# Within a pair, the product of a22 between the second and the third sum's instead of ahead of both

## The chip, the cores and the metric

The kernel runs on one core of one Trainium2 chip. The metric is device time in microseconds (us), taken over whole executions. The kernel before takes 1060.31 us (median of 3 runs, 1059.55 to 1061.11).

## The reference

One decoder layer on 512 tokens and 16 learned meta tokens, width 2048, all in fp32. What is computed, cut to what matters here:

```python
u = rms_norm(h, norm_w)                       # h: 528 x 2048
proj = u @ w_in                               # w_in: 2048 x 8192, eight parts of 1024 columns
sb_q, sb_k, sb_v, sb_g, df_q, df_k, df_v, df_g = split(proj)
# 8 heads of stick-breaking attention (sb): a = exp(log_beta + tail sum of log_keep), masked; out = a @ v
# 8 heads of differential attention (df): q, k normed and rotated, w = softmax1 - lam * softmax2; out = w @ v
mixed = concat(sb_o * silu(sb_g), rms_norm(df_o) * silu(df_g))
y = mixed @ w_out                             # w_out: 2048 x 2048
h = h + y
```

The two projections are the bulk of the matrix work.

## The kernel before

**Pairs.** The 64 column blocks (128 columns each) of the input projection are taken two at a time as 32 pairs, numbered 0 to 31, the 16 blocks of the output projection as 8 pairs, 32 to 39. A pair is a product of a 2 x 2 block matrix of weights (two column blocks times the two halves of the depth; its four quarters are a11, a21, a12, a22) with a 2 x 2 block matrix of activations (two halves of the depth, two halves of the tokens). It is done with seven block products instead of eight, on sums of quarters: the activations' sums are made once (`combine`), the weights' for each pair. Pairs 2 to 31 (the in-pairs) and 33 to 39 (the out-pairs) go this way; pairs 0, 1 and 32 are multiplied directly.

**The seven products.** `STEPS` (L56) gives for each its PSUM bank and its activations: s1 into bank d, a11 into bank a, a12 into b, a22 into c, s2 and s3 *added onto* bank a, s4 into e. In the trace the banks of pair 34 are pj34a to pj34e. Each product is 8 blocks of depth (7 in the out-pairs), each three matmuls of 256 or 264 columns (high by high, high by low, low by high parts: L279, L280, L281). After a11, ScalarE copies bank a (ev_a, L470); after s2, VectorE reads bank a and writes u4 = a + m5 (ev_u, L523); after s3, ScalarE copies it again (ev_g). The first matmul of s3 writes bank a, so it has to wait for ev_u. The pair's results are formed with banks b, c, a and e by `final` (L478); in the out-pairs `final` first adds 6 matmuls each (`plain`, tiles w..pl) for the part of the depth left over.

**Order of products.** `uses(s)` (L227) lists them: s1, a11, then s4 of the pair before, a12, a22, s2, s3. `proj_pair` walks it. After each block of depth it ticks the attention work of the head before, which is interleaved with the products. The framework then plans all instructions with a simulated timeline: among those that it holds to be ready it takes the earliest in program order, with a boost for what stands under `hp`, and so fixes each engine's order and which buffer a tile takes. Engines then run their queues in that order.

**Weights.** `w_loads` loads the quarters of the next pair from SyncE's queue into tiles of 512 KB (wr.., six buffers). For the in-pairs the sums are made by accumulating DMAs from GpSimd's queue (`w_add`, L174), in place: s1 = a21+a22, then s2 = that + a11, then s4 = that + a12, in the tile of a21; s3 = a11+a21 in that of a11. The DMA of a sum is issued after the split of what stood in its tile before (`NEXT`): s2's after s1's split, s4's after s2's. For the out-pairs GpSimd adds (`OUT_SUMS`, L220): s1 in a21's tile, s2 in a11's, s3 = s2 - a22 in a21's, s4 in a12's. `w_prep` splits a weight tile into a high and a low part, two units each: ScalarE writes the high part (L124, w.._h), VectorE the low one (L125, w.._l), into a ring of four units. `preps` runs ahead of the products and prepares in the order of the same `uses(s)`, so the ring holds two products' weights. In the trace w34a_h stands for any of a11, a12, a22 and w34s_h for any sum.

Of the kernel before, what the change touches and what calls it, by code (L numbers as in the profile page):

```python
# [82 lines left out]
def build(nc, tc, ctx, hT, win, wout, wpl, xT, prm, cst, out):  # L83
# [142 lines left out]

    def uses(s):  # L227

        o = [(s, which) for which in ("s1", "a11", "a12", "a22", "s2", "s3")]
        if s - 1 > 1 and s - 1 not in (last_in, last_in + 1):  # L230
            o.insert(2, (s - 1, "s4"))
        if s in (last_in, len(plan) - 1):
            o.append((s, "s4"))
        return o

    def preps():


        for s in range(1, len(plan)):
            if s == last_in + 1:  # L240
                continue
            while (s, "a22") not in raw or (s, "a12") not in raw:
                yield
            if s == 1:
                for quads, _ in ROWS:
                    for u in range(2):
                        for which in quads:
                            w_half(s, which, u)
                            yield
                continue  # L250
            for t, which in uses(s):
                w_prep(t, which)
                yield
                if which == "a12" and s > last_in:
                    w_prep(s, "pl")
                    yield
# [195 lines left out]
    def proj_pair(s, dst, base=None, done=None):  # L452
# [50 lines left out]
        for t, which in uses(s):  # L503
            if which == "s4":
                if t == s:
                    yield from last()
                else:
                    yield from carried.pop(t)
                continue
            yield from multiplied(which)  # L510
            x = STEPS[which][0]
            if which == "a11":
                m1 = copied(x, "a")
                onto_base(0, 0, m1)
            elif which == "s1":
                m5 = copied(x, "d")
                onto_base(1, 1, m5)
            elif which == "a12":
                yield from final(x, 0, 0, m1)
            elif which == "s2":  # L520
                u4 = ev("u")
                with hp(offset=600):
                    V.tensor_tensor(u4, bank(x), m5, op=ALU.add)  # L523
                onto_base(0, 1, u4, ALU.subtract)
            elif which == "s3":
                u3 = copied(x, "g")
                onto_base(1, 0, u3, ALU.subtract)
                yield from final("c", 1, 0, u3, ALU.subtract)
                yield from final(x, 1, 1, m5)
# [436 lines left out]
    s = last_in + 1  # L966
# [142 lines left out]
```

## Time and profile before

| what | us |
|---|---|
| median of 3 runs | 1060.31 |
| the profiled execution's own time | 1060.54 |
| its span (first to last instruction) | 1058.8 |
| TensorE busy (PE) | 1017.8 |
| VectorE busy (DVE) | 832.1 |
| ScalarE busy (ACT) | 631.1 |
| GpSimd busy (POOL) | 432.2 |

The busy time of an engine is the union of its instructions. Of TensorE, ends of matmuls are modelled: a matmul of 256 columns shows some 0.28 us while the next starts 0.12 us later, so a short gap between starts does not show as idle time. The in-pairs run from some 60 to 845 us, pair 32 and the last attention from there to some 900, the out-pairs from there to the end.

### The profile page before, as it was taken

How to read it: one execution, taken by the hardware profiler on the slowest of the kernel's cores; microseconds unless marked ns; L12 is line 12 of the kernel's file. 1: busy time of each engine (PE TensorE's matmuls, PEld its weight loads, DVE VectorE, ACT ScalarE, POOL GpSimd, SP SyncE). 2: the span in 40 equal slices, each digit the busy share in tenths (PEclk: the TensorE clock that was granted, in tenths of full speed). 3: DMA queues.
4: the chain of work that ended last, by engine and by line, in shares of the span. 5: the costliest groups of instructions: out<-in, count | busy, mean ns of one | idle time of the engine just before them, and what ended most of it. 6: DMA issues, size and time to landing. Idle time of an engine off the chain costs nothing. (4 is left out here: it accounts for less than half of the span.)

```text
span 1058.8 us, 21804 instructions
## 1 busy us (share of the span) xinstructions
PE 1017.8 (96%) x8263; PEld 997.4 (94%) x8263; DVE 832.1 (79%) x1577; ACT 631.1 (60%) x1226; POOL 432.2 (41%) x374
## 2 busy tenths in 40 slices
PE   8899999999999999999999999999999987999998
PEld 7899999999999999999999999999999986899998
DVE  5978877878787878787868796878687999578766
ACT  9836665666565566566745674666566665344443
POOL 3544224323422352244224422432243265477574
PEclk9999999999999999999999999999999988999999
DMA  9346685777677767767776767676768535345431
GB/s 338 84 112 141 165 191 141 180 168 190 148 182 173 176 161 170 180 153 169 169 172 167 172 159 180 154 183 158 192 140 210 135 105 164 113 131 161 156 121 36
DMA packets 55113, 169.28 MB, mean 160 GB/s; under 512 B 6368, under 2 KB 7904, under 8 KB 55008
## 3 DMA queue, kind: packets, MB, share of 16 engines
q0 software_dynamic: 17280, 62.92, 33.9%
q1 hardware_dynamic: 37584, 104.96, 28.7%
q8 instruction: 65, 1.06, 0.4%
q14 instruction: 40, 0.33, 0.1%
q10 hardware_dynamic: 144, 0.01, 0.0%
HBM read 160.00 MB, written 7.86 MB: 159 GB/s over the span
## 5 line engine op out<-in xcount | busy, mean ns | idle before, releaser
L838 ACT ACTIVATE df_p<-df_s,df_mx,df_q_r 128x144 f32<-128x144 f32 (+3 forms) x64 | 40.2, 628 | 13.5 <-DVE df_mx L836 11.9
L749 POOL TENSOR_TENSOR df_o_r<-df_o_m,mhalf 128x8 f32<-128x8 f32 x8 | 13.7, 1714 | 57.3 <-DVE df_o_m L745 57.3
L710 DVE TENSOR_TENSOR_SCAN sb_r<-sb_k,ones 128x144 f32<-128x144 f32 (+3 forms) x32 | 29.3, 916 | 7.6 <-ACT sb_k L707 6.5
L835 DVE TENSOR_REDUCE df_mx<-df_s 128x1 f32<-128x144 f32 (+3 forms) x64 | 32.0, 500 | 3.3 <-PE df_s L833 3.3
L830 PE MATMUL df_s<-df_dk,df_qs 128*128 128x264 f32 (+3 forms) x80 | 24.4, 313 | 7.7 <-ACT df_p L838 7.7
L124 ACT ACTIVATE sb_ah<-sb_at 128x512 fp32r<-128x512 f32 (+4 forms) x40 | 18.0, 449 | 20.2 <-PE sb_at L631 18.5
L124 ACT ACTIVATE df_ah<-df_at 128x512 fp32r<-128x512 f32 (+4 forms) x40 | 17.7, 444 | 18.2 <-PE df_at L631 17.9
L707 ACT ACTIVATE sb_k<-sb_s,nrqs 128x144 f32<-128x144 f32 (+3 forms) x32 | 17.3, 541 | 17.6 <-PE sb_s L704 14.2
L830 PEld LDWEIGHTS df_s<-df_dk,df_qs 128*128 128x128 f32 x80 | 15.0, 188 | 10.4 <-ACT df_p L838 10.4
L631 PE MATMUL sb_at<-ident,a_all 128*128 128x128 f32 x112 | 20.8, 278 | 4.1 <-DVE a_all L712 4.1
L833 PE MATMUL df_s<-df_dk,df_qs 128*128 128x264 f32 (+3 forms) x80 | 23.7, 297 | 0.0
L125 DVE TENSOR_TENSOR sb_al<-sb_at,sb_ah 128x512 fp32r<-128x512 f32 (+4 forms) x40 | 20.0, 500 | 3.8 <-ACT sb_ah L124 3.4
L749 POOL TENSOR_TENSOR df_k_r<-df_k_m,mhalf 128x10 f32<-128x10 f32 x8 | 19.2, 2404 | 8.6 <-DVE df_k_m L748 8.5
L125 DVE TENSOR_TENSOR df_al<-df_at,df_ah 128x512 fp32r<-128x512 f32 (+4 forms) x40 | 19.8, 497 | 0.3
L733 POOL TENSOR_TENSOR df_q_sh<-df_q_sh,sin_t 128x512 f32<-128x512 f32 x8 | 12.4, 1552 | 18.3 <-DVE df_q_sh L732 18.3
L631 PE MATMUL df_at<-ident,a_all 128*128 128x128 f32 x112 | 19.8, 272 | 0.0
L712 DVE TENSOR_TENSOR a_all<-sb_b,sb_r 128x143 f32<-128x143 f32 (+3 forms) x32 | 18.0, 563 | 1.9
L279 PE MATMUL pj<-uth,w32a_h 128*128 128x256 f32 x56 | 16.1, 305 | 3.4 <-DVE o31b L487 3.4
L838 ACT ACT_TABLE_LOAD x7 | 9.0, 1283 | 17.5 <-DVE df_mx L836 17.5
L708 ACT ACTIVATE sb_b<-sb_s,rqs 128x144 f32<-128x144 f32 (+3 forms) x32 | 17.3, 539 | 2.8 <-DVE a_all L712 2.8
L631 PEld LDWEIGHTS sb_at<-ident,a_all 128*128 128x128 f32 x112 | 13.1, 137 | 5.8 <-DVE a_all L712 4.5
L832 PE MATMUL df_s<-zid,mdf 128*128 128x256 f32 x64 | 18.0, 281 | 0.0
(2599 smaller groups left out, 5354.3 us busy)
## 6 DMA issues: line engine op xcount, KB each, us to landing
xr<-in_xT SPq DMA_DIRECT2D x16, 256.0 KB, 3.4
out_dram<-xr SPq DMA_DIRECT2D x13, 256.0 KB, 2.0
wr0a<-in_win SPq DMA_DIRECT2D x8, 256.0 KB, 5.2
wr1a<-in_win SPq DMA_DIRECT2D x4, 512.0 KB, 7.3
wr2a<-in_win SPq DMA_DIRECT2D x4, 512.0 KB, 4.0
wr2a<-in_win POOLq DMA_DIRECT2D x4, 512.0 KB, 5.6
wr3a<-in_win SPq DMA_DIRECT2D x4, 512.0 KB, 3.5
wr3a<-in_win POOLq DMA_DIRECT2D x4, 512.0 KB, 7.1
```

The costliest lines, as they stand in the source:

```text
L124: S.activation(hi, src, AF.Copy)
L125: E.tensor_tensor(lo, src, hi.bitcast(F32), op=ALU.subtract)
L631: PE.transpose(pt[:kk, i * P:(i + 1) * P], a_t[i][:, b * P:b * P + kk], ident)
L707: S.activation(sview(keep, i), view, AF.Sigmoid, scale=nrqs[:, i:i + 1])
L710: V.tensor_tensor_scan(run[:, ::-1], keep[:, ::-1], ones_t.to_broadcast([P, n]), 1.0, op0=ALU.mult, op1=ALU.mult)
L712: V.tensor_tensor(a_t[i][:, :n - 1], beta[:, :n - 1], run[:, 1:], op=ALU.mult)
L749: G.tensor_tensor(r, m, mhalf[:, :2 * nb].rearrange("p (a c) -> p a c", c=2), op=ALU.pow)
L830: PE.matmul(o, qst[c][:, qs], dk[:, c, cs], start=True, stop=False)
L832: PE.matmul(diag[0], mdf, diag[1], start=False, stop=False)
L833: PE.matmul(o, qst[c][:, qs], dk[:, 2 + c, cs], start=False, stop=True)
L835: V.tensor_reduce(mxn, view, axis=AX.XY if i == 3 else AX.X, op=ALU.max, negate=True)
L838: S.activation(sview(pt, i), view, AF.Exp, bias=mxn, scale=rqn[:, i, c:c + 1], accum_out=sums[:, c:c + 1])
```

## The change

One line of `uses`: a22 moves behind s2.

```diff
     def uses(s):

-        o = [(s, which) for which in ("s1", "a11", "a12", "a22", "s2", "s3")]
+        o = [(s, which) for which in ("s1", "a11", "a12", "s2", "a22", "s3")]
         if s - 1 > 1 and s - 1 not in (last_in, last_in + 1):
             o.insert(2, (s - 1, "s4"))
```

As `preps` and `proj_pair` both walk this list, the order of the products and the order in which their weights are prepared change together: s2's weights are split one product earlier, a22's one later, the sum s4 (which waits for s2's split) can be issued earlier, and the tile of a22 is let go later. It holds for the 30 in-pairs and the 7 out-pairs. No instruction is added or taken away.

## Rows read from the trace of the kernel before

**Rows 1.** The page's busy times by engine: us, share of the span, instructions.
```profile
PE 1017.8 (96%) x8263; PEld 997.4 (94%) x8263; DVE 832.1 (79%) x1577; ACT 631.1 (60%) x1226; POOL 432.2 (41%) x374
```
**Rows 2.** Busy time by stretch: us, PE, PEld, DVE, ACT, POOL, granted clock, DMA share, GB/s.
```profile
410.00:510.00 100.00, 98.69 (x820) 97.14 (x820) 78.27 (x160) 61.78 (x120) 35.16 (x30) 1.00 0.72 171
...
942.00:963.00 21.00, 20.46 (x171) 20.29 (x171) 16.37 (x20) 9.56 (x18) 15.52 (x14) 1.00 0.50 161
```
**Rows 3.** Waits of TensorE: who waited for whom, us in total, times, longest.
```profile
PE df_s L830 <- ACT df_p L838: 7.7, 13, 0.9
...
PE pj31e L279 <- ACT w31s_h L124: 1.7, 1, 1.7
...
PE pj36a L279 <- DVE ev_u L523: 1.2, 1, 1.2
...
PE pj35a L279 <- DVE ev_u L523: 1.1, 1, 1.1
...
PE pj33a L279 <- ACT w34s_h L124: 0.6, 1, 0.6
```
**Rows 4.** Timeline of TensorE where s3 follows s2 (out-pairs 34, 35, 36).
```profile
941.49 0.28 PE L281 MATMUL pj34a<-uth,w34s_l 128*128 128x256 f32 x1
942.38 0.36 PE L279 MATMUL pj34a<-uth,w34s_h 128*128 128x256 f32 x1 [0.61 <-DVE ev_u L523]
...
963.90 0.36 PE L279 MATMUL pj35a<-uth,w35s_h 128*128 128x256 f32 x1 [1.06 <-DVE ev_u L523]
...
985.56 0.36 PE L279 MATMUL pj36a<-uth,w36s_h 128*128 128x256 f32 x1 [1.19 <-DVE ev_u L523]
```
**Rows 5.** Timeline of TensorE where s3 follows s2 in in-pair 18.
```profile
508.12 0.28 PE L281 MATMUL pj18a<-uth,w18s_l 128*128 128x264 f32 x1
508.24 0.28 PE L279 MATMUL pj19d<-uth,w19s_h 128*128 128x256 f32 x1
...
509.55 0.45 PE L830 MATMUL df_s<-df_dk,df_qs 128*128 128x400 f32 x1 [0.92 <-ACT df_p L838]
...
511.31 0.28 PE L279 MATMUL pj18a<-uth,w18s_h 128*128 128x264 f32 x1
```
**Rows 6.** Timeline of VectorE: splits of pair 34's a22, s2 and pair 35's s1.
```profile
934.55 2.72 DVE L125 TENSOR_TENSOR w34a_l<-wr34a,w34a_h 128x512 fp32r<-128x512 f32 x2
...
938.13 0.54 DVE L125 TENSOR_TENSOR w34s_l<-wr34a,w34s_h 128x384 fp32r<-128x384 f32 x1
...
943.44 0.83 DVE L125 TENSOR_TENSOR w35s_l<-wr35a,w35s_h 128x512 fp32r<-128x512 f32 x1 [1.21 <-ACT w35s_h L124]
```
**Rows 7.** SyncE's queue: the load of pair 35's a21.
```profile
937.34 0.33 SPq L157 DMA_DIRECT2D wr35a<-in_wout  x1
```
**Rows 8.** Timeline of TensorE: the first matmul of pair 35's s1.
```profile
944.94 0.28 PE L279 MATMUL pj35d<-uth,w35s_h 128*128 128x256 f32 x1
```
**Rows 9.** Pair 18's sums s2, then s3: issue (count, ns, us) and time to landing.
```profile
L174 POOL DMA_DIRECT2D wr18a<-in_win x1: 1214/1214/1214, 488.7 to 488.7; - x1
DMA to landing us min/median/max: 9.0/9.0/9.0
...
L174 POOL DMA_DIRECT2D wr18a<-in_win x1: 888/888/888, 490.0 to 490.0; - x1
DMA to landing us min/median/max: 11.3/11.3/11.3
```
**Rows 10.** Timeline of ScalarE and TensorE: first split and first matmul of pair 18's a22.
```profile
496.15 0.63 ACT L124 ACTIVATE w18a_h<-wr18a 128x512 fp32r<-128x512 f32 x1 [0.50 <-PE pj17e L280]
...
500.39 0.29 PE L279 MATMUL pj18c<-uth,w18a_h 128*128 128x264 f32 x1
```
**Rows 11.** Timelines of GpSimd, ScalarE, VectorE around the last in-pair's s4.
```profile
838.06 0.87 POOL L174 DMA_DIRECT2D wr31a<-in_win  x1 [4.34 <-DVE vl L125]
...
843.66 0.63 ACT L124 ACTIVATE w31s_h<-wr31a 128x512 fp32r<-128x512 f32 x1 [2.66 <-DMA wr31a<-in_win]
...
844.32 0.74 DVE L125 TENSOR_TENSOR w31s_l<-wr31a,w31s_h 128x512 fp32r<-128x512 f32 x1 [1.20 <-ACT w31s_h L124]
```

## The prediction

> **What bounds the kernel now.** I read four views. First the page's busy times [rows 1]: TensorE is busy 96% of the span, VectorE 79%, the others less. The reader is to see there that only time in which TensorE does not start matmuls can be won by an order, and that this is about 4% in all. Second the stretches [rows 2]: in a stretch of in-pairs TensorE is busy 98.69 of 100 us, in the stretch of one out-pair 20.46 of 21, both at a granted clock of 1.00, the upper of its two levels. So in both stages TensorE is the bound, no clock is to be won back there, and what is left is short waits. Third who TensorE waits for [rows 3]. The rows to see are those of pj33a to pj39a: a matmul into bank a of an out-pair waits for ev_u, the read of that same bank after s2. Seven out-pairs have it; pairs 36 and 35 with 1.2 and 1.1 us idle, the other five with 0.6 (of pairs 33 and 39 the view names a weight split, which ran at the same moment and is not the cause; the place is the same). No in-pair is in that list with ev_u. Fourth the timeline at those places. In pair 34 the last matmul of s2 starts at 941.49 and the first of s3 at 942.38 [rows 4]. In in-pair 18 the last of s2 starts at 508.12, and the next matmul, 0.12 later, belongs to the s1 of pair 19; s3 comes at 511.31 [rows 5]. There the planner has already put other work between s2 and s3. The wait for ev_u is thus paid in the out-pairs alone.
>
> **The change part by part.**
>
> *The wait between s2 and s3, out-pairs.* Normal steps are 0.12 us from start to start (508.12 to 508.24, [rows 5]). Pair 34 takes 942.38 - 941.49 = 0.89, so it loses 0.77, which is its shown idle 0.61 plus 0.16. Pairs 33, 37, 38 and 39 show the same 0.6 and lose the same 0.77; pair 35 loses 1.06 + 0.16 = 1.22, pair 36 1.19 + 0.16 = 1.35 [rows 4]. Sum: 5 x 0.77 + 1.22 + 1.35 = 6.42 us. After the change a22's 21 matmuls stand there, 21 x 0.12 = 2.5 us of work into another bank, and the longest gap seen between s2's last start and s3's first is 1.35 + 0.12 = 1.47. The wait is covered whole. Ahead of s2 stands now a12, 2.5 us too, which covers the copy of bank a after a11 as a12 and a22 did together.
>
> *What is late next.* The next pair's s1. In pair 35 the low part of its first unit ends at 943.44 + 0.83 = 944.27 [rows 6] and its first matmul starts at 944.94 [rows 8]: 0.67 to spare. If TensorE comes 0.77 earlier, it finds 0.10 missing. Five pairs (35 to 39) have such a predecessor, so I take 5 x 0.10 = 0.5 off: 5.9 us. This part lies between 0 (all of it turned into that wait, rival 1) and 6.42.
>
> *The in-pairs.* Nothing of the kind is to be won, since the place is filled. What moves there: s2's weights are needed where a22's are now. Pair 18: the sum is issued at 488.70 and lands 9.0 us later, at 497.7 [rows 9]; ScalarE now splits a22's first unit at 496.15, and TensorE starts that product at 500.39 [rows 10]. ScalarE would stand 1.5 us at the sum. Then 0.63 for the high part [rows 10] and some 0.7 for the low one (the rows of VectorE's splits have 0.54 to 0.83, [rows 6]): ready at 499.0, 1.4 before TensorE wants it. On TensorE's path I put 0. What is queued behind the waiting split on ScalarE are copies and exponentials of the attention, whose scores TensorE reads or makes room for. Upper bound: all 1.5 us pass on to TensorE, once in each of 7 heads, 10.5 us lost. The other way, TensorE's waits for the exponentials in the in-pairs, 7.7 us in 13 places [rows 3], lie in s2 and s1 of just these pairs, and another interleaving may shorten or lengthen them; I bound that gain by half of it, 4 us, and take 0, as the same instructions wait for the same predecessors.
>
> Here the Trainium skill has a price for the accumulating DMA: the page "DMA: Bandwidth & Descriptors", section "Anatomy of one DMA", fits a GpSimd-issued transfer with 2.0 us plus the bytes over 436 GB/s, which for 512 KB gives an estimate of 3.2 us. By that price the sum would land at 491.9, no split would wait, and rival 2 would fall away. The trace does not agree: the row has 9.0, and it decides.
>
> *The last in-pair.* Its s4 sum is issued at 838.06, ScalarE stands 2.66 us for its landing, TensorE 1.7 [rows 3, 11], and VectorE idles 1.20 ahead of its part. After the change s2's split, which releases that DMA, comes a product earlier, so the landing does too. Behind that part stand pair 32's splits in VectorE's queue, so I count its idle 1.20 as won (bounds: 0 and TensorE's 1.7).
>
> *The loads and queues.* The tile of a22 is let go a product later, so one load of SyncE's queue can start later. In the in-pairs it feeds a product a whole pair away. In the out-pairs it may be the load on the path; that is rival 1. GpSimd's queue keeps its order but for s4's sum, which moves ahead; GpSimd is busy 41% and idle in front of such DMAs (4.34 in [rows 11]). No queue gets more to do.
>
> Sum, against the profiled execution's own 1060.54 (its span is 1058.8; the median of the runs is 1060.31, 0.2 lower): 1060.54 - 5.9 - 1.2 = 1053.4 us.
>
> **The rivals.**
>
> *Rival 1: the next pair's load takes the place of the wait.* The load of pair 35's a21 starts at 937.34 [rows 7], right when VectorE ends the second split of pair 34's a22, 934.55 + 2.72 = 937.27 [rows 6]: it seems to wait for that tile. After the change this split stands where s2's second is, which ends at 938.13 + 0.54 = 938.67, 1.4 later. With 0.67 to spare and TensorE 0.77 early, s1 of the next pair would then start 1.5 us late in five pairs: 7.5 lost against 6.42 and 1.2 won, 1060.4. Against it: s2's tile (a11's) is let go earlier by the same step, and the planner can give that one to the load. The Trainium skill, "Perfetto Trace Analysis", section "Optimization Strategy", says that the same gap again and again on the busiest engine can mean too few buffers for the next tile. By that rule the gap stays under another name, this rival; the rows name a read of the bank itself, so I give it little. Chance 0.10.
>
> *Rival 2, slower: the second sum comes too late in the in-pairs.* Its place is ScalarE's queue at s2's first split in the pairs that I take to stand as 18 does, those of even number (15 of them, 2 to 30). Pair 18's s3 sum, issued 1.3 us behind s2's, took 11.3 us [rows 9]. If s2's takes as long, 2.3 more, the spare 1.4 is used up and TensorE stands 0.9 us in each: 15 x 0.9 = 13.5 lost, 1066.9. For it: s4's sum now follows closer on the two, and the planner does not know real landing times. Against it: s2's stays the first of the two in its queue. It decides from 7.1 / 15 = 0.5 us a pair, a landing 1.9 us later than today. Chance 0.18.
>
> *Rival 3: the change does not do what it says.* The planner reorders by readiness; [rows 5] show a whole part of a product moved. Where it holds s2's weights to be late it takes a22 first, as now, and the out-pairs keep their wait: 1060.5. Against it: in the out-pairs the sums need no DMA. Chance 0.10.
>
> **How the numbers follow.** The forecast, 1053.4, has a chance of 0.62; its own range is 1049.4 to 1057 (4 us of gain in the in-pairs on one side, half of the 7.1 gone on the other). Range at 8 in 10: 1049 at the low end; at the high end it takes in rivals 1 and 3 and 1.5 us for unlike interleavings, 1062, and leaves out rival 2. About 0.2% (2.1 us) is what a measurement of this kernel can tell from no change. Faster by more than that: the forecast, 0.62. Within: rivals 1 and 3, 0.20. Slower: rival 2, 0.18.
>
> **What would show it.** Right: no wait of pj33a to pj39a for ev_u; an out-pair of 20.3 us from s3 to s3, where 34 to 35 takes 963.90 - 942.38 = 21.5 with its 1.22 [rows 4]; the last in-pair's e bank without its 1.7 us; the in-pairs' stretches at 98.7 of 100 still. Rival 1: waits of pj35d to pj39d for w..s_l. Rival 2: ScalarE waiting for the DMA wr.. in many in-pairs, with TensorE waiting for w..s. Rival 3: c before the second a in the timeline. The forecast is wrong if the stretch from 110 to 810 us changes its length by over 3 us, whatever the out-pairs do.

## The result, and the profile after

Over four runs of each on one chip the changed kernel takes 1048.34 us (1046.51 to 1049.84), the kernel before 1060.64 (1059.55 to 1061.11). The ratio is 0.9881, 95% interval 0.987 to 0.9893: 12.6 us less (12.3 between the medians). The forecast was 1053.4, and its range ended below at 1049, 0.7 above the median measured. The direction was right; the gain is 1.7 to 1.8 times the 7.1 us forecast.

The page's busy times of the changed kernel, as [rows 1]:

```profile
PE 1013.4 (97%) x8263; PEld 994.0 (95%) x8263; DVE 828.8 (79%) x1577; ACT 627.7 (60%) x1226; POOL 438.3 (42%) x374
```

The same 8263 matmuls and a span that is 14.0 us shorter (1044.7): TensorE had less time without a matmul. (This profiled run is the fastest of its four, 1.8 below their median.)

Two stretches of the changed kernel, columns as in [rows 2]; the second lies 9 us earlier, as the out-pairs 34 and 35 do (their b banks start 8.3 and 9.2 earlier):

```profile
410.00:510.00 100.00, 99.28 (x826) 97.87 (x825) 78.34 (x163) 62.20 (x123) 35.49 (x30) 1.00 0.71 174
...
933.00:954.00 21.00, 21.00 (x180) 21.00 (x179) 15.01 (x20) 9.56 (x18) 16.55 (x13) 1.00 0.52 164
```

The out-pair is busy all of its 21 us, as forecast. But in the in-pairs, which the forecast left at 98.7, TensorE is busy 0.59 us more in this stretch of 100, and 3.24 us more from 110 to 810 us (694.79 beside 691.55). That is the first sign of what was missed.

TensorE's waits in the changed kernel, as [rows 3]:

```profile
PE df_s L830 <- ACT df_p L838: 3.0, 6, 0.5
...
PE pl L280 <- DVE utl L125: 1.3, 1, 1.3
...
PE pj7a L281 <- DVE w7s_l L125: 0.8, 1, 0.8
```

No wait of pj33a to pj39a for ev_u is left, and none of pj31e. Of the 13 waits of score groups (df_s, 7.7 us) seven are gone. New are waits of the second sum for the low half of its weights (w..s_l) in pairs 7, 11, 15, 19, 23, 27 (0.8 in pair 7, 0.3 in pair 19, 0.2 in the others).

TensorE's timeline in the changed kernel where s2 of out-pair 35 ends, as [rows 4]:

```profile
950.13 0.28 PE L281 MATMUL pj35a<-uth,w35s_l 128*128 128x256 f32 x1
950.24 0.28 PE L279 MATMUL pj35c<-uth,w35a_h 128*128 128x256 f32 x1
...
953.20 0.28 PE L279 MATMUL pj35a<-uth,w35s_h 128*128 128x256 f32 x1
```

a22 starts 0.11 after s2's last matmul, s3 follows 2.96 later, and nothing waits.

Where the time went I read from three lengths on TensorE's timeline, before and after, in every kernel: the in-pairs (first matmul into bank a of pair 2 to that of pair 30), the middle (from there to that of pair 34: last in-pair, last attention, first out-pair) and the out-pairs (from there to the last matmul of pj39e). Lengths, not positions, because several profiled runs reached pair 2 some 1.5 us later, most of them at a mean clock of 0.93 instead of 0.97 between 40 and 90 us. Differences to the kernel before in us; "gain" is 1 less the ratio, times the time before, from all runs:

```
kernel            in-pairs  middle  out-pairs   gain (ratio, 95%)
changed              -3.7    -4.6     -6.2      12.6 (0.9881, 0.987-0.9893)
e1_out_only           0.0    -2.1     -6.1       7.0 (0.9934, 0.9921-0.9948)
e2_in_only           -3.8    -2.8     -0.3       5.4 (0.9949, 0.9936-0.9961)
e13_type1            -3.7    +0.6     -0.4       4.0 (0.9962, 0.9948-0.9976)
e4_type2              0.0    -1.4     -0.1       0.2 (0.9998, 0.9989-1.0008)
e3_last_in_only       0.0    -3.2     +0.2       3.4 (0.9968, 0.9957-0.998)
e18_old33            -3.7    -2.5     -6.2      11.5 (0.9892, 0.9879-0.9906)
e5_own_bank          -5.3    -3.8     -5.8      14.4 (0.9864, 0.9851-0.9878)
e6_swap              +2.2    -4.9     -2.2       3.6 (0.9966, 0.9953-0.9978)
e10_swap33            0.0    -4.0     -0.7       4.7 (0.9956, 0.9944-0.9967)
e9_both33            -4.0    -7.5     -6.9      18.0 (0.983, 0.9817-0.9843)
e11_allmix           -9.5    -8.2     -7.1      22.7 (0.9786, 0.977-0.9802)
e14_no_pool         -10.5    -7.7     -6.2      22.4 (0.9789, 0.9774-0.9805)
e17_old_no_pool      -0.5    -3.4     -0.5       3.7 (0.9965, 0.9951-0.9979)
e15_mult_v           -7.7   -10.0     -7.0      23.5 (0.9778, 0.9765-0.9792)
e16_mix_v            -5.6    -9.4     -7.1      21.0 (0.9802, 0.9788-0.9815)
```

The forecast had 0, -2.0 (1.2 and 0.77) and -5.1 in these columns for the changed kernel. By its own sign of being wrong, over 3 us in the in-pairs whatever the out-pairs do, the 3.7 decide against it.

Each row of lengths is one execution. In the in-pairs e1, e3, e4 and e10 agree with the kernel before to 0.05 us. The middle varies more: e13 keeps the old order in all of it and has +0.6. The profiled execution of the changed kernel is the fastest of its four; its columns sum to 14.5 where all runs give 12.6, so of its middle up to 2 us may be that execution's own.

### The profile page after: what moved, and what is told of

It reads as the page before. It is cut to its first block, busy times and chain, and to the rows that moved or that the text cites. A ratio compares the mean times of both kernels' runs of the same rounds, so it can differ in the third digit from the quotient of the medians.

```text
span 1044.7 us, 21830 instructions
## 1 busy us (share of the span) xinstructions
PE 1013.4 (97%) x8263; PEld 994.0 (95%) x8263; DVE 828.8 (79%) x1577; ACT 627.7 (60%) x1226; POOL 438.3 (42%) x374
## 5 line engine op out<-in xcount | busy, mean ns | idle before, releaser
L124 ACT ACTIVATE df_ah<-df_at 128x512 fp32r<-128x512 f32 (+4 forms) x40 | 17.7, 442 | 16.5 <-PE df_at L631 16.1
L749 POOL TENSOR_TENSOR df_k_r<-df_k_m,mhalf 128x10 f32<-128x10 f32 x8 | 16.4, 2045 | 14.3 <-DVE df_k_m L748 14.2
L846 DVE SCALAR_TENSOR_TENSOR a_all<-df_p,df_cf,df_p 128x144 f32<-128x144 f32 (+3 forms) x32 | 20.5, 641 | 0.3
L281 PE MATMUL pj<-uth,w32a_l 128*128 128x256 f32 x56 | 16.4, 304 | 2.8 <-DVE w32a_l L125 2.8
```

The lines of the kernel that those rows point to most:

```text
L124: S.activation(hi, src, AF.Copy)
L749: G.tensor_tensor(r, m, mhalf[:, :2 * nb].rearrange("p (a c) -> p a c", c=2), op=ALU.pow)
L846: V.scalar_tensor_tensor(a_t[i][:, :n], pts[1], cf, pts[0], op0=ALU.mult, op1=ALU.add)
```

## The theories, and the experiments

**T1**: the whole gain comes from one wait, that of s3's first matmul for the read of bank a after s2. In the out-pairs TensorE idles it. In the in-pairs the planner fills it with attention matmuls that it pulls ahead, and these are not ready themselves, so the wait is paid under another name. **T2**: the gain comes from sums and loads that land earlier. **T3**: any other order would have reshuffled the in-pairs as much.

**The order in the out-pairs alone (e1), and in the in-pairs alone (e2).**

```diff
-        o = [(s, which) for which in ("s1", "a11", "a12", "a22", "s2", "s3")]
+        new = s > last_in
+        o = [(s, which) for which in (("s1", "a11", "a12", "s2", "a22", "s3") if new else ("s1", "a11", "a12", "a22", "s2", "s3"))]
```

(e2 has `new = s <= last_in`.)

> The new order (s2 ahead of a22) only in the eight out-pairs 32 to 39; the in-pairs 2 to 31 keep the old one. Theory T1 (the whole gain is the time in which a matmul into bank a after s2 waits for the read of that bank; in the out-pairs TensorE idles it, in the in-pairs it is paid by score groups that the planner pulls ahead): the out-pairs give what they gave in the changed kernel, 8 us from the traces (last matmul -14.6, less -6.4 at the first b bank of pair 33), the in-pairs nothing: about 1060.5 - 8 = 1052.5, range 1051.5 to 1054.5. Pair 31's wait for s4's sum (1.7 us) stays. Theory T2 (the gain comes from sums and loads that land earlier) expects the same out-pairs, since no sum there needs a transfer, only if it is T1 that holds there; with T2 alone the out-pairs give at most the 6.4 us of idle time. Theory T3 (any other order in the in-pairs would have reshuffled them) says nothing here.

> The new order only in the in-pairs 2 to 31; the out-pairs keep the old one. T1: the in-pairs gain 4.5 us as in the changed kernel (first b bank of pair 31 at -4.5) and pair 31's end 1.9: 1060.5 - 6.4 = 1054.1, range 1053 to 1057; the waits of pj33a to pj39a for the bank's read stay. If part of the in-pairs' gain was handed back in pair 32's attention, less: up to 1059. The two gains, of the out-pairs alone and of the in-pairs alone, should add to the change's 12.3 if they are independent.

Measured 1054.07 beside 1061.07, and 1055.98 beside the same: 7.0 and 5.4 us. Their sum is 12.4 against the change's 12.6, so the two halves add, and the in-pairs with the last of them hold over 40% of the gain. With the old order in the in-pairs their length is that of the kernel before to 0.01 us.

**A bank of its own for s3, in the old order (e5).**

```diff
-         "s2": ("a", T2), "s3": ("a", T3), "s4": ("e", B22)}
+         "s2": ("a", T2), "s3": ("g", T3), "s4": ("e", B22)}
...
-            more = which in ("s2", "s3")
+            more = which == "s2"
```

> The old order (a12, a22, s2, s3), but s3 accumulates in a bank of its own, so its first matmul no longer waits for the read of bank a after s2. What it leaves out: the sum of s1 and s2 that bank a held is not added into s3's result. All loads, sums and products stay where they were. T1: the gain of the changed kernel comes without its order: no wait of pj33a to pj39a for the bank's read, 6.4 to 8 us in the out-pairs, and in the in-pairs s3 follows s2 at once, the score groups come later, TensorE's waits for ACT df_p fall from 7.7 us in 13 places to 3 or less, 3 to 5 us: 1048 to 1052. Pair 31's 1.7 us stay. T2 (sums and loads that land earlier): nothing in the in-pairs, 6.4 in the out-pairs at most: 1054. T3 (a chance reshuffle): the in-pairs change either way by a few us.

Measured 1046.47, 14.4 us less: as much as the change within the intervals, with no product moved. In every pair the first matmul of s3 now starts 0.12 after the last of s2. TensorE's waits for the score groups in this kernel:

```profile
PE df_s L830 <- ACT df_p L838: 2.9, 6, 0.5
```

They fall from 7.7 in 13 places to 2.9 in 6, as in the changed kernel, and the in-pairs gain 5.3. Taking away the hazard on the bank (the wait of a write for the read ahead of it) gives both halves of the gain; T2 falls as its chief cause. One expectation failed: the wait of pj31e, which was to stay at 1.7, is gone; e3 takes that up. The Trainium skill, "Perfetto Trace Analysis", section "Optimization Strategy", says that a gap that repeats can mean too little SBUF or PSUM for the next tile. The prediction weighed that for the weight tiles. This run agrees with the rule for the PSUM bank: one bank more takes the gap away, though only by leaving out a sum that the kernel needs.

**Another order with the two sums still side by side (e6).**

```diff
-        o = [(s, which) for which in ("s1", "a11", "a12", "a22", "s2", "s3")]
+        o = [(s, which) for which in ("s1", "a11", "a22", "a12", "s2", "s3")]
```

> Another order, in which s2 and s3 still stand side by side: s1, a11, a22, a12, s2, s3, so a22 and a12 are swapped and nothing stands between the two sums. T1: nothing is won, 1060.5 within 2 us; the waits of pj33a to pj39a for the bank's read stay at 0.6 to 1.2, and TensorE's waits for ACT df_p in the in-pairs stay near 7.7 us. T3 (any reshuffle of the in-pairs would have moved them as much, and by chance): the first b bank of pair 31 moves by 3 us or more, either way, though s2 and s3 stay side by side. T2: a12's tile is let go later, a22's earlier; the loads move and the time may move with them by a few us.

Measured 1057.28: 3.6 less, where T1 expected nothing within 2. As T1 has it, pj34a to pj38a still wait 0.6 to 0.7 for ev_u, and in pair 25 the gap between s2 and s3 is 1.37 us long, where it was 1.38. But two things failed. The in-pairs lost 2.2 us, so an order alone does move them, and it takes e5 and e13 to rule T3 out as the cause. And the waits of score groups for df_p, which were to stay near 7.7, are not listed at all; in their stead six df_at matmuls wait 0.6 each, and pj7d, pj11d, ..., pj27d 0.9 each for w..s_l. So the fall of those waits alone is no sign of T1. The out-pairs gained 2.2, of which the gaps between s2 and s3 give some 1.2 (three other matmuls stand in each now); the rest I can't place. The middle gained 4.9. That is a gain of another kind, which e10 takes up.

**Which in-pairs (e13, e4).** The pairs of a head run as numbers 4n to 4n + 3. TensorE's timeline of the kernel before, in-pair 25, shows a second place beside that of [rows 5]:

```profile
690.11 0.28 PE L281 MATMUL pj25a<-uth,w25s_l 128*128 128x256 f32 x1
690.46 0.38 PE L654 MATMUL sb_o<-sb_ah,vh 128*128 128x256 f32 x1
690.90 0.39 PE L654 MATMUL sb_o<-sb_al,vh 128*128 128x256 f32 x1
...
691.49 0.28 PE L279 MATMUL pj25a<-uth,w25s_h 128*128 128x256 f32 x1
```

The last matmul of s2 starts at 690.11, the first of s3 at 691.49, and between them stand three sb_o matmuls and two of pj26d. At a step of 0.12 they would have started at 690.23 and 690.58 at the latest; they lose 0.23 and 0.32, one after sb_ah, one after sb_al. In the changed kernel the same group lies inside s3 and nothing waits:

```profile
689.10 0.28 PE L281 MATMUL pj25a<-uth,w25s_l 128*128 128x256 f32 x1
689.22 0.28 PE L654 MATMUL sb_o<-sb_ah,vh 128*128 128x256 f32 x1
689.34 0.28 PE L279 MATMUL pj25a<-uth,w25s_h 128*128 128x256 f32 x1
```

So e13 takes the new order in pairs 4n + 1 alone, e4 in pairs 4n + 2 alone (`s % 4 == 2`, eight pairs with pair 2; the line of `o` is that of e1):

```diff
+        new = s <= last_in and s % 4 == 1
```

> The new order only in the in-pairs 5, 9, ..., 29 (number 4n + 1), seven of them; all else old. T1, made sharper by the traces: with s3 held back by the read of bank a, the planner pulls the group of three sb_o matmuls of pair 24's attention forward into the gap between s2 and s3 of pair 25 (690.11 to 690.46 to 690.90), where it waits for its own operands: 0.23 + 0.33 = 0.56 us lost a head. With a22 in the gap the group comes later and nothing waits. So these pairs alone give 7 x 0.6 = 4.2 us, nearly the whole of the in-pairs' 4.5; TensorE's waits for ACT df_p stay at 7.7 in 13 places. Time: before less 4.2, range 3 to 5. T3 (chance reshuffle): any amount, either sign. If instead the gain sits where the score groups were (pairs 4n + 2), as T1 first had it, nothing is won here.

> The new order only in the in-pairs 6, 10, ..., 30 (number 4n + 2), seven of them; all else old. T1: the score group df_s that was pulled into the gap comes later, its 1.08 us wait goes (TensorE's waits for ACT df_p fall from 7.7 in 13 places to about 3 in 6), but the lead is handed back in the next pair, where the low half of a split comes late (0.6 a head in the changed kernel and in the one with a bank of its own): 7 x 0.2 = 1.3 us won in all, range 0 to 3. If the wait for the low half belongs to the new order of pair 4n + 3 itself, and is not what the lead runs into, the whole 0.85 to 0.95 a head stays: 6 to 6.6 us.

e13 measured 4.0 us (4.2 expected) and -3.7 in the in-pairs: these seven pairs alone give as much as the change gives in all the in-pairs. They are 0.69 shorter each, 4.9 in all, and 1.2 comes back in the pairs behind them, whose score groups now wait 9.0 in 13 places where I expected 7.7. The gap between s2 and s3 of pair 25, where the sb_o group stood, holds no lost time any more. e4 measured 0.2, nothing. Its waits of score groups did fall, to 3.3 in 6 places, but others came:

```profile
PE pj19c L282 <- DVE w19a_l L125: 0.4, 1, 0.4
```

From pair 6 on, the first matmul into bank a of a pair 4n + 3 comes 0.8 to 1.8 us earlier against that of the pair ahead of it. Five score matmuls that now stand in pair 4n + 3 make 0.6 of this, the rest is a lead; and over the whole of the in-pairs the shift is back at 0.0. The lead is handed back in full (1.3 us more than I expected), in this kernel at the low half of a22's weights, with the old order in that pair. It is not the new order of pair 4n + 3 that waits, but the earlier arrival.

**What hands it back (e14, e17).** VectorE's and GpSimd's timelines of the changed kernel in pair 23:

```profile
625.72 3.18 DVE L125 TENSOR_TENSOR w23s_l<-wr23a,w23s_h 128x512 fp32r<-128x512 f32 x2 [0.62 <-ACT w23s_h L124]
```
```profile
625.31 1.31 POOL L600 TENSOR_TENSOR o21a<-o21a,df_sg 128x512 f32<-128x512 f32 x1 [7.29 <-ACT df_sg L599]
626.56 1.80 POOL L584 TENSOR_TENSOR o22a<-o22a,rstd 128x528 f32<-128x528 f32 x1
```

Two low halves take 3.18 us while GpSimd multiplies beside them. The experiments leave the two multiplications out, in the changed kernel (e14) and in the kernel before (e17):

```diff
-        G.tensor_tensor(raw_v, raw_v, rstd, op=ALU.mult)
...
-        G.tensor_tensor(gf, gf, sg, op=ALU.mult)
```

> The changed kernel without two multiplications on GpSimd: that of the gates by their sigmoid, and that of the values by rstd (both left out of what is computed). Question: in the pairs 4n + 2 the new order wins 0.85 to 0.95 us, and pair 4n + 3 hands it back while TensorE waits for the low half of a split. In the changed kernel that split takes VectorE 3.18 us for two instead of 1.38, while GpSimd runs these multiplications (625.31 to 628.36). If that is what hands it back: TensorE's waits of pj7a, pj11a, ... for w..s_l go, and 0.6 a head more is won: the changed kernel less 4, about 1044.5. If the split is late for its own place in the queue (ScalarE's table load and sigmoid ahead of the high half): the waits stay, within 1 us of the changed kernel.

> The old order in every pair, without the two multiplications on GpSimd (the gates by their sigmoid, the values by rstd: both left out of what is computed). If they hurt only where the new order's lead runs into the split that they slow: little is won in the in-pairs, 0 to 2 us (the score group pulled ahead still waits, near 7.7 us in 13 places, and the sb_o group too), and 0 to 3 around pair 32: about 1058. If they cost any order the same 9.8 us: 1051, and the changed kernel's further gain without them says nothing of the order.

In e14 the same two low halves take 1.30:

```profile
621.15 1.30 DVE L125 TENSOR_TENSOR w23s_l<-wr23a,w23s_h 128x512 fp32r<-128x512 f32 x2 [0.62 <-ACT w23s_h L124]
```

In the in-pairs all waits for w..s_l are gone, and they gain 10.5 us, 6.8 more than in the changed kernel: 7 heads by 0.97. From pair 7 on the pairs 4n + 3 are now 0.6 longer than before, which is the five score matmuls alone. In the old order the same omission gives 0.5 in the in-pairs, and the score groups wait as before (7.8 in 13 places). So the two belong together: what the new order wins in pairs 4n + 2 is real, and GpSimd's multiplications hand it back. I expected 4 us more from e14 and it was 9.8; 3.1 of these lie in the middle, where e17 has 3.4 without the new order, and are not the change's.

**The last in-pair alone (e3)**: `new = s == last_in`.

> The new order only in the last in-pair, 31; all else old. The prediction gave it 1.2 us (bounds 0 and 1.7); the trace of the changed kernel says 1.9 (last matmul of pj31e at -6.43 where its first b bank stood at -4.52). T1 and T2 both expect TensorE's wait of pj31e (1.7) to go, since s4's sum is issued a product earlier: before less 1 to 2 us, with pair 32's attention, which VectorE bounds, perhaps giving part of it back. If the 1.9 was only the in-pairs' lead seen late: nothing.

Measured 3.4 us (interval 2.1 to 4.6), by the trace 3.2, over the 1 to 2 expected. The sum of s4 is issued 2.9 us earlier (835.18, before 838.06), and the wait of pj31e falls to 0.4. The last matmul of pj31e comes 1.6 earlier, and the last one of pj33d, behind the last attention, 3.2: what VectorE bounds there did not give the lead back, but doubled it. No run shows why.

The late landing alone does not make that wait. In the kernel before, pj31e's first matmul stands between s2 (its last matmul starts at 842.21) and s3, pulled ahead like the groups of T1:

```profile
844.34 0.39 PE L279 MATMUL pj31e<-uth,w31s_h 128*128 128x256 f32 x1 [1.66 <-ACT w31s_h L124]
...
846.83 0.28 PE L279 MATMUL pj31a<-uth,w31s_h 128*128 128x256 f32 x1
```

In e5, where s3 has its own bank, ScalarE stands even longer for that sum, which lands 1.65 us behind the start of s2's last matmul (1.37 before). But pj31e comes behind s3 and waits for nothing:

```profile
839.59 0.63 ACT L124 ACTIVATE w31s_h<-wr31a 128x512 fp32r<-128x512 f32 x1 [3.18 <-DMA wr31a<-in_win]
...
841.71 0.28 PE L279 MATMUL pj31e<-uth,w31s_h 128*128 128x256 f32 x1
```

**Pair 33 (e18, e10, e9).** e18 has the new order everywhere but in the first out-pair, e10 the old order everywhere but there, with a22 ahead of a12; e9 has the new order and in pair 33 s1, a11, a22, s2, a12, s3. The edit of e9:

```diff
+        first = s == last_in + 2
+        o = [(s, which) for which in (("s1", "a11", "a22", "s2", "a12", "s3") if first else ("s1", "a11", "a12", "s2", "a22", "s3"))]
```

> The new order everywhere but in pair 33, the first out-pair, which keeps the old one. If pair 33 gains only its own wait for the bank's read (0.77): the changed kernel plus 0.8, about 1049.2. If its order also makes the other 1.2 us that the changed kernel gained there (the granted clock there was 0.69 for a stretch before and 1.00 after): plus 1.9, about 1050.3. If the gain there came from the earlier arrival alone: as the changed kernel, 1048.4.

> Everything old but pair 33, the first out-pair, which takes s1, a11, a22, a12, s2, s3. In the run with a22 and a12 swapped everywhere, pair 33 was 5 us shorter than before (first matmul into bank a of 33 to that of 34: -2.14 less 3.00), and the idle 1.5 us ahead of the products of pl, with the lower granted clock that followed it in the kernel before (0.69 from 910 to 915 us), was not there. If that belongs to pair 33's own order (a22's work fills the wait for the last head's output): before less 5, range 3.5 to 6. If it came from the order of the in-pairs ahead of it: nothing. T1 says nothing on it, as s2 and s3 stand side by side here.

> The new order everywhere but in pair 33, which takes s1, a11, a22, s2, a12, s3: a22 ahead of the wait for pl, and a12 (with pl's products) between s2 and s3. If the two gains are independent: the changed kernel's 12.3 us, less the 1.9 that it had in pair 33, and 5 to 6 in its place: before less 15.5 to 16.5, about 1044.5; the bank's read stays covered. If the changed order has already taken what the swap gives in pair 33: the changed kernel's time, about 1048.5. If a12 so late delays the next pair (its result is the first that leaves): slower than the changed kernel.

e18 gains 11.5, 1.1 less than the change, with intervals that overlap; by the traces 2.1 less in the middle. Here are the stretches (columns as in [rows 2]) of e18, then of the changed kernel:

```profile
900.00:905.00 5.00, 3.30 (x18) 2.05 (x17) 2.98 (x7) 1.44 (x3) 1.23 (x2) 1.00 0.26 92
905.00:910.00 5.00, 4.91 (x27) 4.66 (x28) 2.38 (x7) 0.63 (x1) 2.14 (x2) 0.66 0.33 105
```
```profile
900.00:905.00 5.00, 3.94 (x34) 3.70 (x32) 3.27 (x8) 2.03 (x5) 1.17 (x2) 1.00 0.29 92
905.00:910.00 5.00, 3.27 (x23) 2.86 (x24) 3.76 (x6) 0.33 (x1) 2.85 (x3) 1.00 0.53 159
```

Both idle at the products of pl, 1.5 us and more. In e18, as in the kernel before (0.69 from 910 to 915), a stretch at a lower mean clock follows, in the changed kernel none. Less 0.77 for the bank's wait, 1.3 of the 2.1 us are left, which I put down to that stretch by subtraction alone. In e18 twelve matmuls from 906.50 on start 0.21 apart instead of 0.12, some 1.1 us; but the changed kernel waits 1.3 more at pl (for utl), so the account doesn't close. Nor is the stretch shown to belong to pair 33's order: with the old order there e2 and e13 have it too (0.66), but e4 does not (1.00 from 900 to 920), and its middle, with the new order in pair 30 alone, is 2.0 shorter than that of e13. Why the clock stays up in some is open. That pair 33 gains some 2 us is seen a second time in e1, where it takes 27.88 us instead of 29.86 (first matmul into bank a to that of pair 34).

e10 gains 4.7 (5 expected): a22's matmuls fill the idle time ahead of pl. e9 gains 18.0, more than the 15.5 to 16.5 expected. In it TensorE is busy all the time from 890 to 920 us, from 895 on at a clock of 1.00.

**a12 between the sums, in every pair (e11).** Beside e6 one thing differs: a12 stands behind s2 instead of ahead of it.

```diff
+        o = [(s, which) for which in ("s1", "a11", "a22", "s2", "a12", "s3")]
```

> Every pair takes s1, a11, a22, s2, a12, s3: the product between the two sums is a12's, and a22's stands ahead of both. T1 (any product into another bank fills the gap): no wait of pj33a to pj39a for the bank's read, the in-pairs gain 3.5 to 4.5 as in the changed kernel, the out-pairs 6 to 6.5 as there, and pair 33 the 5 to 6 that it gave when it alone had this order: 1043 to 1045, as that kernel. If it matters which product fills (a22's tile let go earlier, a12's later, the first result of a pair later): the loads or the attention show it, and the time is nearer the changed kernel's 1048.5 or above.

Measured 1038.28: 22.7 us less than before, 19 less than e6. For T1 either product fills the gap: no wait for ev_u is left, and the out-pairs gain 7.1 (6 to 6.5 expected). But it matters to the rest which one does: the in-pairs gain 9.5 instead of the 4 expected. In e11, as in e6, no wait of a score group for df_p is listed at all. That surplus I had not foreseen, and no run shows its cause; where it shows is that a head has 0.4 us of waits for w..s_l left in it, where the changed kernel has 0.64, and 0.27 for the score group, where that has 0.68 (both read from the steps of TensorE in pairs 22 and 23).

**The multiplications on VectorE (e15, e16).** e15 is e9 with the two multiplications on VectorE, e16 is e11 with them.

```diff
-        G.tensor_tensor(raw_v, raw_v, rstd, op=ALU.mult)
+        V.tensor_tensor(raw_v, raw_v, rstd, op=ALU.mult)
...
-        G.tensor_tensor(gf, gf, sg, op=ALU.mult)
+        V.tensor_tensor(gf, gf, sg, op=ALU.mult)
```

> The same two multiplications kept, but on VectorE instead of GpSimd, on top of the changed order with pair 33 in the order s1, a11, a22, s2, a12, s3 (that kernel: ratio 0.983 to the kernel before, 18 us less). If GpSimd's multiplications cost VectorE 0.75 and 1.1 us where they run beside its splits, VectorE is better off with two operations of some 0.7: 2 to 4 us less, about 1040. If VectorE's queue (79% busy) can't take them in time, 1 to 3 us more.

> Every pair in the order s1, a11, a22, s2, a12, s3, and the two multiplications on VectorE instead of GpSimd. The first alone measured a ratio of 0.9786 to the kernel before, the second on top of the changed order with pair 33 swapped 0.9778, where that order alone had 0.983. If the two take away different waits they add: 0.973 to 0.974, about 1033. If both take away the same one (the low half of a split that comes late in pair 4n + 3; the first run has 0.2 to 0.4 a head left of it): 0.977 to 0.979, about 1037.

e15 measured 1037.73, 5.5 us less than e9 by the ratios: VectorE is better off with two more operations of its own. e16 measured 1039.78, 1.7 more than e11 by the ratios, with intervals that overlap: the two gains don't add, and neither expectation (1033 or 1037) was met. Both e11 and e15 beat the changed kernel by 10 to 11 us; their intervals overlap.

## Why the prediction was wrong, step by step

**The failed step: "On TensorE's path I put 0" for the in-pairs, with "nothing of the kind is to be won, since the place is filled".** It took the filled gap of [rows 5] as a gap that costs nothing. The row with the price stood in the same group: the score group at 509.55 waited 0.92. I saw it, counted it as a wait for the exponentials, and did not ask why that group stood there. It stood there because s3 could not start: the planner brought other work forward, and a matmul that isn't ready holds up all behind it on TensorE's queue (pj19d's next one, at 510.13). e5 shows it: with the hazard gone and no product moved, s3 follows s2 at once and the in-pairs gain 5.3 us, where the changed kernel's gain 3.7. Bounding the gain by half of 7.7 us was near in size (3.7), but by luck, for the wrong place: e13 shows that the 3.7 come from the sb_o groups of pairs 4n + 1, which my views of one pair, 18, did not hold, while the score groups' waits went and were handed back (e4, e14).

**The wait in the out-pairs**: right. Pairs 34 to 39 had 5.65 of the 6.42 us; they gave 6.2, and e1 gave 6.1 there (the 0.5 above the gaps, some 0.1 a pair, I can't place). From 35 to 38 the first b banks follow at 20.2 us (944.58 and 964.75 in pairs 35 and 36), where 20.3 was forecast. The 0.5 taken off for a late s1 of the next pair did not come: no pj35d to pj39d waits.

**Pair 33**: its term of 0.77 measured 2.1 (changed kernel against e18; 2.0 in e1). What made the rest is open. The stretch at a lower clock that followed its idle time was not in the sum; the prediction said that no clock was to be won back, from two stretches that don't hold pair 33.

**The last in-pair**: 1.2 forecast, 3.2 alone (e3). The sum went by one idle time of VectorE; TensorE's wait gave 1.6 of it, and the work queued behind it, the last attention, gave as much again. The step that failed is the same one: this wait too was that of a matmul pulled into the gap between s2 and s3. In e5 VectorE idles 1.22 as before, and TensorE's wait is gone.

**Rival 1**: not seen; e11 moves both tiles and still gains. **Rival 2**: its wait came (w7s_l 0.8, w19s_l 0.3), but not its cause or its size. In pair 23 ScalarE's split of 625.07 came behind a table load and a sigmoid (623.24 to 625.16), while both its sums had landed by 623.96; VectorE's low half was slow, and it cost no more than the lead. Such slow low halves stood in [rows 6]: 2.72 us for two of pair 34's a22, while GpSimd added from 933.70 to 936.86; the prediction went by the 0.54 to 0.83 of the others. **Rival 3**: not seen; pairs 18, 25 and 35 have the new sequence on TensorE.

## What to carry to other kernels

A gap that a planner has filled is not free: look at what fills it, and if that waits itself, the hazard behind it still costs its time under another engine's name. The test is to remove the hazard (a bank of its own) with no product moved. And when a lead vanishes a stage later, look at which operation takes longer than elsewhere in the trace at that place, not only at who is named as the releaser.

## What the runs showed of the hardware

GpSimd's multiplications of 128x512 and 128x528 slow VectorE's splits beside them: two low halves of 128x512 took 3.18 us with them and 1.30 without (e14), and moving these operations to the busier engine made the kernel 5.5 us faster (e15 beside e9). And some 1.5 us without matmuls in pair 33 was followed by a mean granted clock of 0.66 to 0.69 for some 5 us in four kernels (before, e2, e13, e18), and by none below 1.00 in the changed kernel, with more idle time at the same place, nor in e4; what tells them apart is open.
